# Modulation weights stored by tiles, one block's products moved ahead of the last of them, and a last down projection that alternates its two experts

## The chip, the cores and the metric

The kernel runs on one core of a Trainium2 chip. The metric is the device time of one execution in microseconds (us). The median of three runs before the change is 1856.98 us (1856.57 to 1857.13).

## What is computed

Two layers over 512 latent tokens and 256 context tokens of width 1024, all in float32:

```
for l in range(2):
    mod = silu(c) @ w_ada[l] + b_ada[l]          # 1024 x 6144: shift, scale, gate, twice; the same for c_ctx
    xn  = rms(x) * g1 * (1 + scale1) + shift1
    u   = xn @ w_in[l]                           # q, k, v, gates | conv a, g | fourier
    x   = x + gate1 * (mixers(u) @ w_out[l])     # mLSTM, Conformer convolution, Fourier mixing
    xn2 = rms(x) * g2 * (1 + scale2) + shift2
    # 16 experts, each takes its 64 latent (32 context) tokens of highest affinity
    x   = x + gate2 * sum_e P_e (silu(xs @ Wg[e]) * (xs @ Wu[e])) @ Wd[e] * affinity
return rms(x) * g_final
```

The context rows run through layer 0 in full; layer 1 needs only their keys, values and gates.

## The kernel before

Feature blocks of 128 stand on the partitions, tokens on the free axis. SBUF is one large tile `A` that the kernel divides by hand, with `RA`, `RB` and six `WP` tiles beside it; `PS` is PSUM, eight banks. PE's order is that of the code, written out by hand. The instructions of the other engines are set in order by a scheduler, and each engine runs its own in order. SP issues nearly all weight loads; GpSimd's queue (POOL) issues the modulation weights except the first 16 tiles, the fetches of scan tables (`scr`) and the indirect gathers and scatters.

**Modulation weights.** `w_ada` is 2 x 1024 x 6144. A tile is 128 rows of it by four pieces of 256 columns (512 KB), and in the array as it is given each row of a tile lies in four runs of 1 KB. There are 96 tiles: 16 in `ada_first` (SP, line 309), 32 in `ada0` and 48 in `ada1` (POOL, line 282, in `ada_round`). Four products of 32 columns each (`cs`, lines 284 and 311) take a tile, one for each column group of the array.

**The start.** `ada_first` makes shift and scale for layer 0 in two halves. The first half gives feature blocks 0, 1, 4, 5; the second gives 2, 3, 6, 7. `KORD` sets the blocks' order to match, and `normed` makes each block's two-part normalized input on ACT and DVE (lines 505 to 510). Two columns of `w_in` are multiplied block by block as they come (`steps`, line 490, 12 products a block). Seven of the eight tiles of the second half stand ahead of the first block (`ADP`); `ADF` says after which block the eighth, with the rows and the selection behind it (lines 316 to 325), stands.

**The middle of layer 0.** Around 330 us the output projection begins. SP has by then queued the zeroing of the two accumulators (`accl`, `accc`) and, in memory that this zeroing reads from, the router's weights (`w_router`, line 1104). DVE scales these (line 1108) ahead of its first residual update (line 1177), which frees PE's banks. POOL loads tiles of `w_ada` for layer 1 in the same stretch.

**The experts of layer 1.** Pairs of experts; each of gate, up and down of a pair takes eight 1 MB tiles. 16 buffers hold them, and SP loads a tile when its buffer is free. In `wide` (line 1433) the two experts' products alternate, expert 0 in columns 0 to 63 of the array and expert 1 in 64 to 127. The last pair's down projection is `down_last`: four quarters (`qd`) of 256 output features. In each quarter the products stand in runs of four of one expert (line 1693), with a scatter (`pop(scat)`: two products of line 1498 and DVE's update, line 1499) behind a run. After a quarter ACT and DVE take its half bank out as a high and a low part (lines 1699 and 1700), and two more scatters are queued; `last_sum` adds the squares (line 1675) whose sums (`rows`, line 1683) give the final norm (line 356 on).

A float32 product is two records in the profile, so 16 products of a quarter are 32 records.

Of the kernel before, what the change touches and what calls it, by code (L numbers as in the profile page):

```python
# [15 lines left out]
KB = 8  # L16
# [29 lines left out]
LEARLY = 6  # L46
ADP, ADF = 7, (2, 0, 0, 0)
CR0, CR1 = 0.75, 1.1
# [107 lines left out]
def build(nc, tc, xT, ctxT, params, w_ada, w_gates, w_in, w_out, w_router, w_e_gate, w_e_up, w_e_down,  # L156
# [3 lines left out]
    pe, act, dve, pool, sp = nc.tensor, nc.scalar, nc.vector, nc.gpsimd, nc.sync  # L160


    def body(A, RB, PS, scr, xrow, acc):
# [112 lines left out]
        def ada_round(l, r, ring, bank, eng, firsts=(), some=1):  # L276
            ps = B(bank)
            src = w_ada[l].rearrange("(k p) (r g h c) -> r h k p g c", p=128, r=3, g=4, h=2)
            for hf in range(2):
                for k in range(KB):  # L280
                    w = V(ring.next(), 4, 256)
# [19 lines left out]
        def ada_first(ring, bank, bank2, eng, splits):  # L301

            ps = B(bank)
            src = w_ada[0].rearrange("(k p) (r g h c) -> r h k p g c", p=128, r=3, g=4, h=2)[0]
            p2 = B(bank2)[:, 0:32].rearrange("p (b v g) -> p b v g", b=4, v=2)
# [91 lines left out]
        for l in range(2):  # L397
# [734 lines left out]
            wq = [(w, 2 * q + e, i) for w, q in order for i in range(4) for e in range(2)]  # L1132
            wtiles, wtaken = [], [0]

            def load_experts(firsts=(), most=1000):
                while len(wtiles) < min(wtaken[0] + len(wreg), len(wq), most):
                    w, e, i = wq[len(wtiles)]
                    if last and w is w_e_down and e >= E - 2:
                        t = V(wreg[len(wtiles) % len(wreg)], KB, 256)
                        src = w[l, e, i].rearrange("p (k c) -> p k c", k=KB)  # L1140

                        for k0, k1 in ((0, KB),) if i < 3 else ((0, 4), (4, KB)):
                            sp.dma_start(t[:, k0:k1], src[:, k0:k1])
                    else:
                        t = V(wreg[len(wtiles) % len(wreg)], 2, D)
                        r = sp.dma_start(t, w[l, e, i].rearrange("p (a f) -> p a f", a=2))
                        after(r, firsts)
                    wtiles.append(t)
# [91 lines left out]
            p = B(3)  # L1240
# [216 lines left out]
            def pop(lst, n=1):  # L1457
                for _ in range(min(n, len(lst))):
                    lst.pop(0)()
# [202 lines left out]
            def down_last(p):  # L1662
# [23 lines left out]
                for qd in range(4):  # L1686
                    w = wtiles[wtaken[0]:wtaken[0] + 2]
                    wtaken[0] += 2
                    b = B(o + qd // 2)[:, qd % 2 * 256:qd % 2 * 256 + 256]
                    for k0 in (0, 4):  # L1690
                        for e in range(2):
                            for k in range(k0, k0 + 4):
                                pe.matmul(b[64 * e:64 * e + 64], hT[:, k, 64 * e:64 * e + 64], w[e][:, k],  # L1693
                                          start=k == 0, stop=k == KB - 1, tile_position=(0, 64 * e))
                            pop(scat)
                    pop(scat, 99)
                    c0 = qd * 256
                    h, lo = (YS[:, j, c0:c0 + 256] for j in range(2))
                    act.activation(h, b, AF.Copy, scale=GP[:, 0, p:p + 1])
                    dve.scalar_tensor_tensor(lo, b, GP[:, 0, p:p + 1], h.bitcast(F32), op0=OP.mult, op1=OP.subtract)  # L1700
                    if qd == 2:
                        rows(range(4))
                    scat.extend(last_sum(db) for db in (2 * qd, 2 * qd + 1))
                rows((4, 5))
# [58 lines left out]
def layout(inputs):  # L1763
# [30 lines left out]
    a["params"] = par  # L1794
    a["w_ada"] = f("w_ada")
    a["w_gates"] = wg.reshape(2, 128, KB * 32)
# [48 lines left out]
```

## Time and profile before

| | |
|---|---|
| median of 3 runs | 1856.98 us |
| the profiled execution's own time | 1857.74 us |
| its span (first to last instruction) | 1856.0 us |
| PE busy | 1744.3 us, 94% |
| DVE busy | 627.9 us, 34% |
| ACT busy | 448.5 us, 24% |
| POOL busy | 166.0 us, 9% |
| moved by DMA | 529.59 MB, mean 285 GB/s |

The busy shares are means over stages with different limits, so the stages are read one by one: what PE waits for at the start, around 360 us and at the end, and when the DMA engines have no room left.

### The profile page before, as it was taken

What the parts mean: (1) busy time and instruction counts of PE and PEld (TensorE: products, weight loads), DVE (VectorE), ACT (ScalarE), POOL (GpSimd) and SP (SyncE); (2) the same over time, 40 slices, a digit from 0 to 9 for tenths busy, and PEclk for the clock granted to TensorE, in tenths of its full rate; (3) what the DMA queues carried; (4) which work ended last, traced back from release to release, by engine and by line L of the source; (5) the groups of instructions that cost most, each with busy time, mean ns of one, the idle gap of its engine ahead of it and who ended that gap; (6) DMA issues with size and microseconds to landing.
All of it is one profiled execution on the core that took longest, in us unless ns stands there. A gap on an engine that the chain in (4) does not pass through costs nothing.

```text
span 1856.0 us, 27692 instructions
## 1 busy us (share of the span) xinstructions
PE 1744.3 (94%) x11728; PEld 947.8 (51%) x11728; DVE 627.9 (34%) x1384; ACT 448.5 (24%) x862; POOL 166.0 (9%) x193
## 2 busy tenths in 40 slices
PE   7899999899899999999999989889989999999997
PEld 3678887676333333333233468777644444334433
DVE  4624897323201001001014567956230221121213
ACT  5423354313201101101000553346221001110001
POOL 1122120321101101101100001110000000000000
PEclk8999999899899999999999999999989999999998
DMA  9365344855899999999995112233659999999992
GB/s 346 115 208 193 106 133 137 314 188 209 350 419 402 411 412 403 399 421 391 393 393 217 35 54 79 76 108 129 250 240 421 420 420 421 420 421 420 421 420 99
DMA packets 100668, 529.59 MB, mean 285 GB/s; under 512 B 10176, under 2 KB 21440, under 8 KB 51648
## 3 DMA queue, kind: packets, MB, share of 16 engines
q1 hardware_dynamic: 81920, 459.66, 61.8%
q0 software_dynamic: 18624, 68.17, 11.7%
q8 instruction: 92, 1.51, 0.3%
q14 instruction: 32, 0.26, 0.0%
HBM read 513.10 MB, written 14.68 MB: 284 GB/s over the span
## 4 chain that ended last, share of the span: by engine, by line
PE 70%; DMA 10%; DVE 9%; issue 5%; ACT 2%; SPq 2%; POOL 1%; another core or an unknown queue 0%; DVEq 0%; POOLq 0%; ACTq 0%
PE PS L1433 29%; PE PS L490 16%; PE PS L1443 8%; PE PS L1379 3%; DVE A L1015 2%; PE PS L1498 2%; PE PS L284 1%; PE PS L1693 1%; SPq L309 1%; DMA accc<-A 1%; DMA WP<-w_e_up 1%; DMA A<-w_e_up 1%; DMA A<-w_e_down 1%; DMA A<-w_e_gate 1%; DMA WP<-w_e_gate 1%
## 5 line engine op out<-in xcount | busy, mean ns | idle before, releaser
L490 PE MATMUL PS<-RA,RB 128*128 128x512 f32 (+1 forms) x2352 | 516.4, 367 | 23.6 <-ACT A L973 8.0
L1433 PE MATMUL PS<-A 128*32 128x512 f32 (+1 forms) x2256 | 428.1, 594 | 2.7 <-DMA A<-w_e_up 2.2
L490 PEld LDWEIGHTS PS<-RA,RB 128*128 128x128 f32 x2352 | 379.3, 194 | 99.3 <-issue 20.6
L1433 PE MATMUL PS<-WP,A 128*32 128x512 f32 (+1 forms) x2160 | 373.9, 597 | 0.7 <-DMA WP<-w_e_up 0.7
L1433 PEld LDWEIGHTS PS<-A 128*32 128x32 f32 (+1 forms) x2256 | 128.0, 121 | 224.9 <-issue 213.7
L1433 PEld LDWEIGHTS PS<-WP,A 128*32 128x32 f32 (+1 forms) x2160 | 107.0, 117 | 192.7 <-issue 187.6
L1443 PE MATMUL PS<-WP,A 128*32 128x512 f32 x816 | 112.5, 595 | 0.0
L1015 DVE SCALAR_TENSOR_TENSOR A<-A 128x783 f32<-128x783 f32 (+1 forms) x120 | 107.4, 921 | 0.1
L1499 DVE SCALAR_TENSOR_TENSOR A<-PS,A 128x512 f32<-128x512 f32 x80 | 57.5, 748 | 130.5 <-PE PS L1498 130.5
L1387 ACT ACTIVATE A<-PS,A 128x128 f32<-128x128 f32 x80 | 36.4, 457 | 262.0 <-DVE A L1389 260.8
L1486 ACT ACTIVATE A<-PS 128x512 f32<-128x512 f32 x40 | 23.8, 597 | 306.2 <-PE PS L1485 306.0
L1389 DVE TENSOR_SCALAR A<-PS,A 128x128 f32<-128x128 f32 x80 | 32.6, 409 | 185.8 <-PE PS L1382 93.4
L1443 PE MATMUL PS<-A 128*32 128x512 f32 x656 | 95.3, 607 | 0.0
L422 ACT ACTIVATE RB<-A 128x1024 fp32r<-128x1024 f32 x60 | 63.2, 1057 | 128.4 <-PE PS L490 83.1
L1532 DVE TENSOR_SCALAR A<-PS,A 128x512 f32<-128x512 f32 x6 | 4.5, 750 | 245.6 <-PE PS L1433 245.6
L282 POOL DMA_DIRECT2D A<-w_ada x80 | 60.1, 754 | 211.2 <-PE PS L284 134.2
L1506 DVE SCALAR_TENSOR_TENSOR RB<-PS,A,RB 128x512 fp32r<-128x512 f32 x18 | 13.5, 750 | 163.7 <-ACT RB L1505 162.8
L1379 PE MATMUL PS<-A 128*128 128x128 f32 x512 | 64.0, 285 | 5.0 <-DVE A L1499 4.5
L425 DVE TENSOR_TENSOR RB<-A,RB 128x1024 fp32r<-128x1024 f32 x50 | 60.8, 1221 | 21.0 <-ACT RB L422 20.6
L1379 PEld LDWEIGHTS PS<-A 128*128 128x128 f32 x512 | 61.0, 199 | 12.9 <-DVE A L1499 9.8
L1443 PEld LDWEIGHTS PS<-WP,A 128*32 128x32 f32 x816 | 26.8, 109 | 50.8 <-issue 50.8
L1498 PE MATMUL PS<-RB 128*128 128x512 f32 x160 | 51.7, 431 | 1.0 <-DVE A L1499 0.4
(334 smaller groups left out, 1583.8 us busy)
## 6 DMA issues: line engine op xcount, KB each, us to landing
A<-w_e_gate SPq DMA_DIRECT2D x75, 1024.0 KB, 14.3
A<-w_e_up SPq DMA_DIRECT2D x66, 1024.0 KB, 13.0
WP<-w_e_down SPq DMA_DIRECT2D x63, 1024.0 KB, 14.3
A<-w_e_down SPq DMA_DIRECT2D x63, 1024.0 KB, 16.0
WP<-w_e_up SPq DMA_DIRECT2D x62, 1024.0 KB, 13.0
WP<-w_e_gate SPq DMA_DIRECT2D x53, 1024.0 KB, 14.9
A<-w_ada POOLq DMA_DIRECT2D x80, 512.0 KB, 5.5
A<-w_in SPq DMA_DIRECT2D x44, 512.0 KB, 3.7
```

The costliest lines, as they stand in the source:

```text
L282: after(eng.dma_start(w, src[r, hf, k]), firsts if hf == 0 and k < len(ring.regs) else ())
L422: whi.append(act.activation(h, raw[i], AF.Copy))
L425: wlo.append(eng.tensor_tensor(lo, raw[i], h.bitcast(F32), OP.subtract))
L490: pe.matmul(banks[s][:, :LEN[s]], w[:, k], xin[:, j, k, OFF[s]:OFF[s] + LEN[s]], start=k == k0 and i == 0, stop=k == k1 and i == 2)
L1015: dve.scalar_tensor_tensor(o, i, wcol, o, op0=OP.mult, op1=OP.add)
L1379: pe.matmul(b[:, j], XT[2 + c][:, db * 128:db * 128 + 128], onehots[i][:, c], start=c == 0, stop=c == 3)
L1387: act.activation(dst[:, db], b[:, j], AF.Identity, bias=sh_, scale=sc_)
L1389: dve.tensor_scalar(dst[:, db], b[:, j], sc_, sh_, op0=OP.mult, op1=OP.add)
L1433: pe.matmul(B(o + hf)[c:c + wd, :], lhs(k, e)[:, c % 64:c % 64 + wd], w[e][:, a, hf * 512:hf * 512 + 512], start=k == 0, stop=k == KB - 1, ...
L1443: pe.matmul(B(o + 2)[32 * g:32 * g + 32, :], lhsc(k, e), w[e][:, a, hf * 512:hf * 512 + 512], start=k == 0, stop=k == KB - 1, tile_positio ...
L1498: pe.matmul(b, YS[:, j, db * 128:db * 128 + 128], PM if pm is None else pm, start=j == 0, stop=j == 1)
L1499: dve.scalar_tensor_tensor(X[LAT][:, db], b, MOD[l][:, LAT, 40 + db:41 + db], X[LAT][:, db], op0=OP.mult, op1=OP.add)
```

## The change

`w_ada` is laid out on the host so that a tile is contiguous: 128 rows of 4 KB. Its loads name the same tiles, buffers and queues. At the start the eighth tile of the second half, and what hangs on it, stands after the second feature block's products and not after the first's. In `down_last` the two experts alternate product by product; the scatters stand behind the quarter's evacuation (in the first quarter, where the ones left from the pair before are taken, ahead of it); `rows(range(4))` stands after the fourth quarter's products; and the last quarter's weights are loaded as first halves of both experts, then second halves.

```diff
-ADP, ADF = 7, (2, 0, 0, 0)
+ADP, ADF = 7, (0, 2, 0, 0)
...
         def ada_round(l, r, ring, bank, eng, firsts=(), some=1):
             ps = B(bank)
-            src = w_ada[l].rearrange("(k p) (r g h c) -> r h k p g c", p=128, r=3, g=4, h=2)
+            src = w_ada[l].rearrange("r h k p (g c) -> r h k p g c", g=4)
...
         def ada_first(ring, bank, bank2, eng, splits):
-            src = w_ada[0].rearrange("(k p) (r g h c) -> r h k p g c", p=128, r=3, g=4, h=2)[0]
+            src = w_ada[0, 0].rearrange("h k p (g c) -> h k p g c", g=4)
...
-                        for k0, k1 in ((0, KB),) if i < 3 else ((0, 4), (4, KB)):
-                            sp.dma_start(t[:, k0:k1], src[:, k0:k1])
+                        halves.append((t, src))
+                        if i < 3:
+                            sp.dma_start(*halves.pop())
+                        elif len(halves) == 2:
+                            for k0 in (0, 4):
+                                for t_, s_ in halves:
+                                    sp.dma_start(t_[:, k0:k0 + 4], s_[:, k0:k0 + 4])
...
-                    for k0 in (0, 4):
+                    for k in range(KB):
                         for e in range(2):
-                            for k in range(k0, k0 + 4):
-                                pe.matmul(b[64 * e:64 * e + 64], hT[:, k, 64 * e:64 * e + 64], w[e][:, k],
-                                          start=k == 0, stop=k == KB - 1, tile_position=(0, 64 * e))
-                            pop(scat)
-                    pop(scat, 99)
+                            pe.matmul(b[64 * e:64 * e + 64], hT[:, k, 64 * e:64 * e + 64], w[e][:, k],
+                                      start=k == 0, stop=k == KB - 1, tile_position=(0, 64 * e))
                     c0 = qd * 256
                     h, lo = (YS[:, j, c0:c0 + 256] for j in range(2))
+                    if qd == 0:
+                        pop(scat, 99)
                     act.activation(h, b, AF.Copy, scale=GP[:, 0, p:p + 1])
                     dve.scalar_tensor_tensor(lo, b, GP[:, 0, p:p + 1], h.bitcast(F32), op0=OP.mult, op1=OP.subtract)
-                    if qd == 2:
+                    if qd == 3:
                         rows(range(4))
+                    pop(scat, 99)
                     scat.extend(last_sum(db) for db in (2 * qd, 2 * qd + 1))
...
-    a["w_ada"] = f("w_ada")
+    a["w_ada"] = np.ascontiguousarray(f("w_ada").reshape(2, KB, 128, 3, 4, 2, 256).transpose(0, 3, 5, 1, 2, 4, 6)).reshape(2, 3, 2, KB, 128, 1024)
```

PE's rows in the second quarter of `down_last`, before (L1693 are the quarter's products, `WP1` and `WP2` the weights of expert 0 and expert 1, L1498 a scatter):

```order
L1693 MATMUL PS_70<-WP1_8538,A_63 64x256 x4
L1498 MATMUL PS_70<-RB_64 128x512 x2
L1693 MATMUL PS_70<-WP2_8539,A_63 64x256 x4
L1498 MATMUL PS_70<-RB_64 128x512 x2
L1693 MATMUL PS_70<-WP1_8538,A_63 64x256 x4
L1693 MATMUL PS_70<-WP2_8539,A_63 64x256 x4
```

The same quarter now (the products are L1699, a scatter is L1504; the pair of rows repeats eight times), from the scatters behind the first quarter to the start of the third:

```order
L1504 MATMUL PS_70<-RB_64 128x512 x4
L1699 MATMUL PS_70<-WP1_8538,A_63 64x256
L1699 MATMUL PS_70<-WP2_8539,A_63 64x256
...
L1504 MATMUL PS_70<-RB_64 128x512 x4
L1699 MATMUL PS_70<-WP3_8540,A_63 64x256
L1699 MATMUL PS_70<-WP4_8541,A_63 64x256
```

Runs of four became an alternation, and both scatters of a quarter stand together behind it.

DVE's rows from the up projection of the last pair to the final norm, before (L1700 is the low part of a quarter, L1499 the update behind a scatter):

```order
L1477 TENSOR_TENSOR A<-PS,A 128x512 x2
L1499 SCALAR_TENSOR_TENSOR A<-PS,A 128x512 x4
L1700 SCALAR_TENSOR_TENSOR RB<-PS,A,RB 128x256
L1499 SCALAR_TENSOR_TENSOR A<-PS,A 128x512 x2
L1700 SCALAR_TENSOR_TENSOR RB<-PS,A,RB 128x256
...
L1499 SCALAR_TENSOR_TENSOR A<-PS,A 128x512 x2
L370 RECIPROCAL A<-A 128x4
```

And now (L1707 and L1505 are the same two):

```order
L1483 TENSOR_TENSOR A<-PS,A 128x512 x2
L1505 SCALAR_TENSOR_TENSOR A<-PS,A 128x512 x4
L1707 SCALAR_TENSOR_TENSOR RB<-PS,A,RB 128x256
L1505 SCALAR_TENSOR_TENSOR A<-PS,A 128x512
L1707 SCALAR_TENSOR_TENSOR RB<-PS,A,RB 128x256
L1505 SCALAR_TENSOR_TENSOR A<-PS,A 128x512 x2
L1707 SCALAR_TENSOR_TENSOR RB<-PS,A,RB 128x256
L1505 SCALAR_TENSOR_TENSOR A<-PS,A 128x512
L1707 SCALAR_TENSOR_TENSOR RB<-PS,A,RB 128x256
L1505 SCALAR_TENSOR_TENSOR A<-PS,A 128x512 x4
L370 RECIPROCAL A<-A 128x4
```

Four updates, not two, now stand behind the last low part, and the third low part stands behind the first update of its own quarter's scatters.

PE's rows at the start, before, between the first block's products and the second's (L490 are the blocks' products, L311 the eighth tile's, L319 the selection):

```order
L490 MATMUL PS<-RA,RB 128x256
L490 MATMUL PS<-RA,RB 128x512
L311 MATMUL PS<-A 32x256 [waits DMAHW7_49]
L311 MATMUL PS<-A 32x256 x3
L319 MATMUL PS<-A 128x8 [waits Activation_49]
L319 MATMUL PS<-A 128x8
```

The same rows now stand behind the second block's 12 products, whose first rows follow on the first block's:

```order
L490 MATMUL PS<-RA,RB 128x256 [waits Activation_49]
L490 MATMUL PS<-RA,RB 128x512
L490 MATMUL PS<-RA,RB 128x256 [waits DVE_49]
...
L311 MATMUL PS<-A 32x256 [waits DMAHW7_49]
L311 MATMUL PS<-A 32x256 x3
L319 MATMUL PS<-A 128x8 [waits Activation_49]
```

12 products that wait for ACT and DVE alone moved ahead of the wait for the eighth tile.

## Rows read from the trace of the kernel before

**Rows 1.** Page, part 2: GB/s in 40 equal slices of the span.

```profile
GB/s 346 115 208 193 106 133 137 314 188 209 350 419 402 411 412 403 399 421 391 393 393 217 35 54 79 76 108 129 250 240 421 420 420 421 420 421 420 421 420 99
```

**Rows 2.** Chain that ended last: start us, us, what.

```profile
350.88 7.25 DMA A<-w_router
...
1476.58 20.75 PE PS L1433 x96
...
1767.65 19.85 DMA A<-w_e_up
```

**Rows 3.** Timeline of PE at the start: start us, us, engine, instructions, [idle before <-releaser].

```profile
37.99 2.03 PE L490 MATMUL PS<-RA,RB 128*128 128x256 f32 x10 [0.16 <-DVE RA L510]
41.19 0.64 PE L311 MATMUL PS<-A 128*32 128x256 f32 x8 [1.17 <-DMA A<-w_ada]
...
42.80 8.72 PE L490 MATMUL PS<-RA,RB 128*128 128x256 f32 x48
```

**Rows 4.** Timeline of DVE at the start.

```profile
36.33 1.94 DVE L510 TENSOR_TENSOR RA<-A,RA 128x512 fp32r<-128x512 f32 x4
...
45.71 0.92 DVE L510 TENSOR_TENSOR RA<-A,RA 128x256 fp32r<-128x256 f32 x2 [0.20 <-ACT A L507]
```

**Rows 5.** Timeline around 360 us.

```profile
358.22 0.76 DVE L1108 TENSOR_TENSOR A<-A 128x256 f32<-128x256 f32 x2 [17.59 <-DMA A<-w_router]
...
360.09 2.93 PE L490 MATMUL PS<-RA,RB 128*128 128x256 f32 x9 [4.39 <-DVE A L1177]
```

**Rows 6.** POOL's DMA queue, 320 to 365, 360 to 440, 446 to 481: packets, MB, share.

```profile
q0 software_dynamic: 2016, 7.34, 44.2%
...
q0 software_dynamic: 3400, 12.34, 47.1%
...
q0 software_dynamic: 718, 2.62, 22.9%
```

**Rows 7.** Timeline of the last down projection, all engines.

```profile
1804.02 1.94 PE L1693 MATMUL PS<-A 128*64 128x256 f32 x8
1805.89 0.73 PE L1498 MATMUL PS<-RB 128*128 128x512 f32 x2
1806.73 0.75 DVE L1499 SCALAR_TENSOR_TENSOR A<-PS,A 128x512 f32<-128x512 f32 x1 [3.50 <-PE PS L1498]
...
1810.22 0.38 PE L1693 MATMUL PS<-A 128*64 128x256 f32 x1
1810.28 0.38 PE L1693 MATMUL PS<-WP,A 128*64 128x256 f32 x1
1810.44 0.38 PE L1693 MATMUL PS<-A 128*64 128x256 f32 x1
...
1812.05 0.47 ACT L1699 ACTIVATE RB<-PS,A 128x256 fp32r<-128x256 f32 x1 [7.42 <-PE PS L1693]
1812.56 0.48 DVE L1700 SCALAR_TENSOR_TENSOR RB<-PS,A,RB 128x256 fp32r<-128x256 f32 x1 [2.54 <-ACT RB L1699]
1813.10 1.49 PEld L1693 LDWEIGHTS PS<-WP,A 128*64 128x64 f32 x8 [1.60 <-DVE RB L1700]
...
1839.47 1.29 ACT L1675 ACTIVATE A<-A 128x512 f32<-128x512 f32 x2 [2.01 <-DVE A L1499]
...
1841.90 0.60 ACT L356 ACTIVATE A<-PS 128x512 f32<-128x512 f32 x1 [1.14 <-PE PS L1683]
```

**Rows 8.** SP's issues of the last weights, and the halves' size and median landing time.

```profile
1799.94 4.03 SPq L1143 DMA_DIRECT2D A<-w_e_down  x2
...
A<-w_e_down SPq DMA_DIRECT2D x2, 512.0 KB, 15.0
```

**Rows 9.** Stretches at the end: us, PE, PEld, DVE, ACT, POOL, granted clock, DMA, GB/s.

```profile
1840.00:1845.00 5.00, 2.76 (x12) 1.24 (x12) 1.00 (x6) 1.59 (x4) 0.00 (x0) 0.95 0.00 0
1845.00:1850.00 5.00, 2.04 (x2) 0.50 (x2) 2.77 (x6) 0.00 (x0) 0.00 (x0) 0.50 0.19 70
```

**Rows 10.** Line 1693 alone: ns min/median/max of one, first and last start.

```profile
L1693 PEld LDWEIGHTS PS<-WP,A x96: 132/137/137, 1806.6 to 1835.4; 128*64 128x64 f32 x96
```

More of the change, by code (lines that the diff above doesn't have):

```diff
@@ L1132, in body @@
             wq = [(w, 2 * q + e, i) for w, q in order for i in range(4) for e in range(2)]
-            wtiles, wtaken = [], [0]
+            wtiles, wtaken, halves = [], [0], []
             def load_experts(firsts=(), most=1000):
```

## The prediction

> **What bounds the kernel now.** I read the GB/s row first. From slice 31 to 39 it stands at 420: the experts of layer 1 are fed as fast as the DMA engines go [rows 1]. The chain of waits says who loses time there: through the experts it runs on PE at first, and later on transfers, one of 19.85 us per eight tiles [rows 2]. SP starts a load when a buffer is free and PE frees buffers, so this whole stretch starts where PE's earlier work ends: a microsecond saved before it is a microsecond saved at the end, as long as it is on PE's path. So three places are read apart: the start, the stretch around 360 us, and the last down projection, where the transfers run out and PE, ACT and DVE set the end alone.
>
> **The start.** PE finishes the first block's products at 37.99 + 2.03 = 40.02 and then idles until 41.19, 1.17 us of it for a tile of `w_ada`; from 41.19 to 42.80 the eighth tile, its copy by ACT and its selection take 1.61 us; then products run dense, 48 in 8.72, 2.18 a block [rows 3]. The second block's input is ready at 36.33 + 1.94 = 38.27 [rows 4], so its products can run from 40.02 to 42.2 and cover the wait for the tile (41.15) whole. The 1.61 us stay bare behind them, 42.2 to 43.8. The third block then starts at 43.8 and not at 42.80 + 2.18 = 44.98: 1.17 us saved. What hides the edit is thin: the fifth block's input, ready at 45.71 + 0.92 = 46.6 [rows 4], comes 1.0 later (47.6), and PE wants it at 43.8 + 2 x 2.18 = 48.2, 0.6 us of cover. If tiles of 4 KB rows land sooner, the wait is gone anyway; the two edits do not add up. Bounds: nothing (if the cover fails by 1.2) to 1.2. I take 1.17.
>
> **The modulation weights.** Bytes, queues and buffers stay, only the runs in DRAM grow. Off PE's path this costs and gives nothing: POOL's loads elsewhere are early. On the path it has one place. PE stands 4.39 us until 360.09 behind DVE, which stands behind the router's weights [rows 5]; these took 7.25 us to land for 128 KB [rows 2], as POOL's queue took 44.2% of the DMA engines' time from 320 to 365, 19.9 us, for 7.34 MB, nearly all `w_ada` [rows 6]. A cheaper `w_ada` lets the zeroing and the router's weights land sooner. No row shows `w_ada` in 4 KB rows. From below: POOL's gathers of 4 KB rows cost 22.9% of 35 us x 16 / 718 = 0.179 us a packet, `w_ada` now 47.1% of 80 us x 16 / 3400 = 0.177, both of some 3.6 KB [rows 6]: nothing gained. From above: at 420 GB/s [rows 1] the 7.34 MB take 17.5 us, 2.4 less; and if the chain were quite free, the whole 4.39. A loss I exclude: no transfer grows. The gathers are the nearest row, but they go from row to row at random places, so I take a little more than their nothing: 0.8.
>
> The Trainium skill (DMA: Bandwidth & Descriptors, Specifications) gives 512 B as the smallest transfer that reaches line rate. By that, runs of 1 KB are already there and this term would be 0. The row of the gathers agrees, as far as it goes.
>
> **The last down projection.** Count from the first product, 1804.02. Now four products of one expert take 1805.89 - 1804.02 = 1.87 us [rows 7]. Where a run of one expert meets the next, the two interleave: records of the two buffers start at 1810.22, 1810.28, 1810.44, so a pair of records takes 0.215 us where one expert alone takes 0.23 a record [rows 7]. Line 1433, which alternates throughout, holds that rate: 96 records of 512 columns in 20.75 us, 0.216 each, twice what one column group could do [rows 2]. So a quarter of 32 records takes 16 x 0.215 = 3.44; I take 3.5, against 4 x 1.87 = 7.5.
>
> Then the hand-overs. A scatter takes 0.73 us (two in a row 1.2, as the second starts under the first); its update starts 0.84 after it and takes 0.75; ACT starts 0.1 behind a quarter, DVE 0.51 later, and PE goes on in the same bank 0.54 after that (1812.05, 1812.56, 1813.10) [rows 7]. With DVE's new order:
> - Quarter 0: 0 to 3.5; two old scatters to 4.7; their updates 4.34 to 5.85; low part at 5.87; PE waits for it (same bank) until 6.41.
> - Quarter 1: to 9.91, scatters to 11.1. Quarter 2 has another bank and starts at once: to 14.6, scatters to 15.8, first update 15.44 to 16.19, low part 16.21, PE at 16.75.
> - Quarter 3: to 20.25; four row sums to 21.15; scatters to 22.35; updates to 23.5; squares (1.29 for two [rows 7]) to 24.2. Here the new order costs: the next row sums stand ahead of the last scatters in PE's queue, so scatter 6 starts at 25.1; updates to 27.45, last square 28.15, and the norm 1.14 later (1839.47 + 1.29 = 1840.76 to 1841.90 now [rows 7]): 29.3.
>
> Now the norm starts at 1841.90 - 1804.02 = 37.88. The tail gains 8.6.
>
> Do weights arrive in time? The last half is issued at 1803.6 and lands 15.0 later, at 1818.6, or 14.6 in this count [rows 8]; quarter 3 wants it at 16.75 or later. At 2.5 us per MB before it (420 GB/s), quarter 2's last tile is there at 9.6 for 11.1, quarter 1's at 4.6 for 6.4. Covers of 1.5 us and more; a later tile would cost what it is late beyond that. The order of the halves hides under this and is worth nothing. The tail's bounds: 7.1, if PE's granted clock falls to 1.2 GHz about 3 us earlier than now (it stands at 0.95 and then 0.50 at the end [rows 9]) and the last scatters and sums double; 9.2, if the row sums cost less than 0.9.
>
> **Sum.** 1.17 + 0.8 + 8.6 = 10.6. The profiled execution took 1857.74: 1847.2. It lies 0.76 above the median of the runs, 1856.98, so the forecast for the median is 1846.4.
>
> **Rivals.**
> 1. *The layout gives nothing.* The gathers' price speaks for it. Only the 0.8 is lost: 1847.2.
> 2. *PE's wait at 360 goes whole.* DVE waited 17.59 us for that transfer [rows 5], in a stretch where the queue is full; against it, `w_ada`'s share would have to shrink by a fifth. 4.4 for 0.8: 1842.8.
> 3. *Weight loads bind the alternation.* A product's load of 64 columns takes 0.135 us [rows 10], and 32 of them 4.3 us, more than 3.44. If loads did not overlap across the column groups, each quarter would cost 0.9 more, 3.5 in all: 1849.9. Against it, in the interleaved records two loads pass in 0.215 [rows 7]. The Trainium skill (TensorE: Matmul & The Clock Gate, Part 3, Measured speedup) has three column tiles at 2.38 and not 3 times. At that efficiency an estimate for a quarter is 3.44 / 0.79 = 4.35, and the time about the same; line 1433 here shows none of that loss.
> 4. *The alternation does not overlap at 256 columns, and switching groups costs as a run does now.* Place: the four quarters. Price: 7.5 for 3.5 each, 16 us, so that the tail loses 7.3: 1862.3. It decides from a quarter of 3.5 + 10.6 / 4 = 6.15 us on. The three interleaved records speak against it; for it only that no full quarter of this form has been seen.
> 5. *The change misses its mark*: the rows of the new order show that it is made, so this is left to rivals 1 and 4.
>
> **How the numbers follow.** Forecast 0.60, rivals 1 to 4: 0.15, 0.08, 0.10, 0.05; 0.02 for mixtures that end near no change. The likeliest gives 1846.4, with its own bounds 1844 to 1849.3 (tail 7.1 to 9.2, start 0 to 1.2, middle 0.3 to 2.4). The range takes in rivals 1 to 3: 1842.0 to 1850.5. It leaves out rival 4 and the mixtures. What a measurement can tell from no change is about 0.2%, 3.7 us. All cases but the last two are faster by more: 0.92 after a little for what I have not seen, 0.03 the same, 0.05 slower.
>
> **What would show it.** PE's timeline at the start: no wait for `w_ada` behind the first block, 12 more products there, the second row sums for the gates 1.2 earlier (if the wait stands, the start was wrong). The wait behind the router's weights: 3 to 4.4 us if rival 1 or the forecast is right, gone by rival 2. In the last down projection: 32 records in 3.4 to 3.6 us; PE idle some 1.7 us ahead of the second quarter and 1 us ahead of the fourth, both for DVE's low part; the norm some 29 us behind the first product; no wait for `w_e_down`. A quarter of 4.3 is rival 3, of 7 rival 4. The prediction is wrong most likely in the tail, if a wait for the last weights takes the place of PE's work, or at 360 us, where one transfer's landing decides.

## The result, and the profile after

The changed kernel takes 1848.18 us (median of five executions, 1842.92 to 1849.08), the kernel before 1857.13 beside it (five, 1856.57 to 1861.64): ratio over all executions 0.993, 95% interval 0.9903 to 0.9958 (the two medians alone give 0.9952). It is faster; the forecast was 1846.4, a ratio of 0.9943 to the 1856.98 shown then. The profiled execution takes 1848.78 with a span of 1847.0, 9.0 less than before.

Where these 9.0 us stand is read from stations that both traces have:

| station | before | after | after minus before |
|---|---|---|---|
| second row sums for the gates (L516) | 59.44 | 60.34 | +0.90 |
| PE behind the wait at 360 (L490) | 360.09 | 361.79 | +1.70 |
| an up projection of layer 1 (L1433, now L1439) | 1476.58 | 1476.80 | +0.22 |
| first product of the last down projection (L1693, now L1699) | 1804.02 | 1804.17 | +0.15 |
| final norm (L356) | 1841.90 | 1833.23 | -8.67 |
| end of the span | 1856.0 | 1847.0 | -9.0 |

So between these two executions all of it comes from the tail, and what lies ahead of it gives nothing. The chain of waits of the kernel after (start us, us, what) has the same links as in [rows 2]:

```profile
353.80 6.03 DMA A<-w_router
...
1476.80 20.75 PE PS L1439 x96
...
1767.78 19.86 DMA A<-w_e_up
```

The transfers of layer 1 are as full as in [rows 1], 420 in slices 31 to 39 (page, part 2):

```profile
GB/s 347 112 209 191 106 123 155 301 203 177 341 420 402 410 413 403 404 418 401 391 406 259 35 39 93 62 108 113 239 222 422 420 421 420 420 420 421 420 421 179
```

**The last down projection.** Timeline of the kernel after; L1699 are the products, L1504 scatters, L1505 their updates, L1706 and L1707 the high and low parts, L1689 row sums:

```profile
1804.44 0.38 PE L1699 MATMUL PS<-A 128*64 128x256 f32 x1
1804.44 0.38 PE L1699 MATMUL PS<-WP,A 128*64 128x256 f32 x1
1804.65 0.38 PE L1699 MATMUL PS<-A 128*64 128x256 f32 x1
1804.66 0.38 PE L1699 MATMUL PS<-WP,A 128*64 128x256 f32 x1
...
1807.78 1.20 PE L1504 MATMUL PS<-RB 128*128 128x512 f32 x4
1808.62 1.41 DVE L1505 SCALAR_TENSOR_TENSOR A<-PS,A 128x512 f32<-128x512 f32 x2 [5.23 <-PE PS L1504]
1810.47 3.67 PE L1699 MATMUL PS<-WP,A 128*64 128x256 f32 x32 [1.50 <-DVE RB L1707]
...
1815.20 3.67 PE L1699 MATMUL PS<-WP,A 128*64 128x256 f32 x32
...
1820.77 0.43 PE L1699 MATMUL PS<-WP,A 128*64 128x256 f32 x1 [0.77 <-DVE RB L1707]
...
1833.23 0.60 ACT L356 ACTIVATE A<-PS 128x512 f32<-128x512 f32 x1 [1.14 <-PE PS L1689]
```

Records of the two experts start in pairs 0.215 apart, and the 32 of a quarter take 3.67. Counted from 1804.17, PE goes on at 6.30 behind DVE's low part, at 11.03 without a wait, and at 16.60 behind DVE again; the norm stands at 29.06, where [rows 7] had 37.88. No row here waits for a transfer: SP's last issue of a half is at 1802.61 (1803.6 before, [rows 8]).

```profile
1802.61 0.33 SPq L1149 DMA_DIRECT2D A<-w_e_down  x1
```

**The start.** PE's timeline after, against [rows 3]:

```profile
32.63 0.64 PE L311 MATMUL PS<-A 128*32 128x256 f32 x8 [0.55 <-DMA A<-w_ada]
34.98 1.08 PE L311 MATMUL PS<-A 128*32 128x256 f32 x8 [1.71 <-DMA A<-w_ada]
37.49 1.08 PE L311 MATMUL PS<-A 128*32 128x256 f32 x8 [1.43 <-DMA A<-w_ada]
38.50 5.79 PE L490 MATMUL PS<-RA,RB 128*128 128x256 f32 x24
44.22 0.64 PE L311 MATMUL PS<-A 128*32 128x256 f32 x8
...
60.34 1.50 PE L516 MATMUL PS<-A 128*32 128x256 f32 x16
```

The eighth tile, at 44.22, is waited for no longer: that is the edit. But PE now waits 3.7 us for three tiles ahead of it, and the first 24 products behind them take 5.79, begun at a lower granted clock (0.50 from 35 to 40 us). These waits were not in the forecast.

**Around 360 us.** Timeline, then POOL's queue from 320 to 365 (packets, MB, share), against [rows 5, 6]:

```profile
359.92 0.76 DVE L1108 TENSOR_TENSOR A<-A 128x256 f32<-128x256 f32 x2 [16.61 <-DMA A<-w_router]
...
361.79 2.93 PE L490 MATMUL PS<-RA,RB 128*128 128x256 f32 x9 [5.59 <-DVE A L1183]
```

```profile
q0 software_dynamic: 2016, 7.34, 40.3%
```

The same 7.34 MB take 40.3% where they took 44.2%, and the router's weights land in 6.03 and not 7.25; but PE's wait is longer, 5.59 for 4.39: the zeroing ahead of these weights was issued at 331.72, 2.7 later than before (329.04), PE's own work only some 0.5 later.

### The profile page after: what moved, and what is told of

It reads as the page before. It is cut to its first block, busy times and chain, and to the rows that moved or that the text cites. A ratio compares the mean times of both kernels' runs of the same rounds, so it can differ in the third digit from the quotient of the medians.

```text
span 1847.0 us, 27691 instructions
## 1 busy us (share of the span) xinstructions
PE 1729.1 (94%) x11728; PEld 939.8 (51%) x11728; DVE 626.9 (34%) x1384; ACT 448.3 (24%) x862; POOL 147.8 (8%) x193
## 4 chain that ended last, share of the span: by engine, by line
PE 70%; DMA 11%; DVE 9%; issue 6%; ACT 2%; POOL 1%; another core or an unknown queue 0%; SPq 0%; DVEq 0%; POOLq 0%; ACTq 0%
PE PS L1439 29%; PE PS L490 16%; PE PS L1449 9%; PE PS L1385 3%; DVE A L1015 2%; PE PS L1504 2%; PE PS L284 1%; DMA A<-w_ada 1%; DMA accc<-A 1%; DMA A<-w_e_gate 1%; DMA A<-w_e_up 1%; DMA WP<-w_e_gate 1%; DMA A<-w_e_down 1%; DMA WP<-w_e_up 1%; DMA WP<-w_e_down 1%
## 5 line engine op out<-in xcount | busy, mean ns | idle before, releaser
L490 PE MATMUL PS<-RA,RB 128*128 128x512 f32 (+1 forms) x2352 | 516.9, 367 | 26.0 <-ACT A L973 7.7
L490 PEld LDWEIGHTS PS<-RA,RB 128*128 128x128 f32 x2352 | 379.7, 194 | 101.9 <-issue 20.0
L1439 PE MATMUL PS<-A 128*32 128x512 f32 (+1 forms) x2256 | 427.7, 594 | 2.7 <-DMA A<-w_e_up 2.2
L1439 PE MATMUL PS<-WP,A 128*32 128x512 f32 (+1 forms) x2160 | 372.6, 595 | 0.6 <-DMA WP<-w_e_up 0.6
L1439 PEld LDWEIGHTS PS<-A 128*32 128x32 f32 (+1 forms) x2256 | 127.8, 121 | 225.0 <-issue 214.5
L1439 PEld LDWEIGHTS PS<-WP,A 128*32 128x32 f32 (+1 forms) x2160 | 106.7, 117 | 191.5 <-issue 186.7
L1505 DVE SCALAR_TENSOR_TENSOR A<-PS,A 128x512 f32<-128x512 f32 x80 | 57.3, 747 | 128.9 <-PE PS L1504 128.9
L282 POOL DMA_DIRECT2D A<-w_ada x80 | 42.4, 533 | 221.2 <-PE PS L284 140.6
L1504 PE MATMUL PS<-RB 128*128 128x512 f32 x160 | 50.6, 428 | 1.0 <-DVE A L1505 0.4
```

The costliest lines, as they stand in the source:

```text
L282: after(eng.dma_start(w, src[r, hf, k]), firsts if hf == 0 and k < len(ring.regs) else ())
L490: pe.matmul(banks[s][:, :LEN[s]], w[:, k], xin[:, j, k, OFF[s]:OFF[s] + LEN[s]], start=k == k0 and i == 0, stop=k == k1 and i == 2)
L1439: pe.matmul(B(o + hf)[c:c + wd, :], lhs(k, e)[:, c % 64:c % 64 + wd], w[e][:, a, hf * 512:hf * 512 + 512], start=k == 0, stop=k == KB - 1, ...
L1504: pe.matmul(b, YS[:, j, db * 128:db * 128 + 128], PM if pm is None else pm, start=j == 0, stop=j == 1)
L1505: dve.scalar_tensor_tensor(X[LAT][:, db], b, MOD[l][:, LAT, 40 + db:41 + db], X[LAT][:, db], op0=OP.mult, op1=OP.add)
```

## The experiments

Executions differed more in these groups than in the first one (the kernel before: 1847.88 to 1864.67), so a ratio is to be read with its interval. Positions are those of the one profiled execution of each kernel: the start of the second row sums for the gates (59.44 before), and the norm counted from the first product of the last down projection (37.88 before).

| run | executions | median | before beside it | ratio (95%) | row sums at | norm |
|---|---|---|---|---|---|---|
| tail | 10 | 1846.85 | 1854.72 | 0.9959 (0.9942 to 0.9977) | 65.86 | 29.06 |
| layout | 12 | 1851.68 | 1854.72 | 0.9974 (0.9961 to 0.9988) | 58.56 | 37.87 |
| order | 12 | 1855.22 | 1854.72 | 1.0002 (0.9985 to 1.0019) | 58.29 | 37.87 |
| head | 12 | 1849.62 | 1854.72 | 0.997 (0.9955 to 0.9984) | 57.92 | 37.88 |
| after2 | 6 | 1842.63 | 1856.44 | 0.9935 (0.9913 to 0.9956) | 56.77 | 29.05 |
| hold | 6 | 1840.66 | 1856.44 | 0.9921 (0.9896 to 0.9945) | 56.90 | 29.05 |
| holdt | 6 | 1840.35 | 1856.44 | 0.9922 (0.9902 to 0.9941) | 58.30 | 29.04 |
| runs | 7 | 1846.68 | 1856.44 | 0.9953 (0.9931 to 0.9975) | 58.18 | 33.13 |
| holdb | 12 | 1850.34 | 1855.85 | 0.9971 (0.9959 to 0.9984) | 57.66 | 37.88 |
| hold_mid | 4 | 1836.13 | 1855.85 | 0.9893 (0.9877 to 0.991) | 56.08 | 26.97 |
| hold_end | 5 | 1840.77 | 1855.85 | 0.9922 (0.9908 to 0.9937) | 56.30 | 25.36 |
| old_mid | 4 | 1840.22 | 1856.8 | 0.9913 (0.9893 to 0.9934) | 57.66 | 26.98 |

### Each part alone

**tail**: the edits of `load_experts` and `down_last` alone.

```diff
-                    for k0 in (0, 4):
+                    for k in range(KB):
                         for e in range(2):
...
+                    pop(scat, 99)
                     scat.extend(last_sum(db) for db in (2 * qd, 2 * qd + 1))
```

> The kernel before with the new last down projection alone (alternation, moved scatters and row sums, order of the last halves). Theory A (the whole gain is the tail; the start and the middle gave nothing that reaches the end): the norm 29.1 us behind the first product of the last down projection, against 37.9 before, and a time 8.8 us below the kernel before, ratio 0.9953, so the same as the changed kernel's profiled execution. Theory B (the parts add as predicted, and the profiled execution of the changed kernel lost 2 us of it by chance): 8.6 below, and the changed kernel's median 2 us better than this one.

The norm is at 29.06, and the ratio is worth 7.6 us of 1854.72 (4.3 to 10.8): the tail's 8.8 lies in it. It does not tell whether the rest gives 0 or 2.

**layout**: the three lines of `w_ada` alone.

```diff
-            src = w_ada[l].rearrange("(k p) (r g h c) -> r h k p g c", p=128, r=3, g=4, h=2)
+            src = w_ada[l].rearrange("r h k p (g c) -> r h k p g c", g=4)
```

> The kernel before with the modulation weights laid out by tiles alone. Theory A: in the first 45 us the transfers run at 415 to 420 GB/s instead of 381 to 402, the first half of ada_first's products ends about 3.5 us earlier, but GpSimd's queue then starts its four tiles earlier too and the second half's tiles come no earlier: the second row sums for the gates stand at 59.4 us plus or minus 1 (before 59.4), the time is that of before within 1 us. Theory B: the start gains 1.2 us (no wait for the eighth tile) and the middle 0.8: 2 us below the kernel before, second row sums at 58.2.

A falls here: the time is 4.8 us lower (2.2 to 7.2), more than B's 2 too. Its one profile shows 0.9 of it at the row sums.

**order**: `ADF` alone.

```diff
-ADP, ADF = 7, (2, 0, 0, 0)
+ADP, ADF = 7, (0, 2, 0, 0)
```

> The kernel before with the eighth tile behind the second block alone, the weights in the old layout. Transfers at the start are as before, so both theories want the second row sums for the gates 1.2 us earlier, at 58.3 us. Theory A: most of that is swallowed before the last stage (a stretch at the lower clock level between 95 and 100 us that ends at the same time, waits on transfers at 235 and 310 us): 0 to 0.6 us below the kernel before. Theory B: 1.2 us below.

The row sums are 1.15 earlier, as both theories wanted; the time is that of before, within 0.2%, which does not tell the theories' 0 to 0.6 and 1.2 us apart.

**head**: layout and order, without the tail.

> The kernel before with layout and order, the last down projection as before. Theory A: the start is that of the changed kernel, second row sums at 60.3 us, PE waiting 3 to 4 us for tiles of the second half between 31 and 38 us; first product of the last down projection at 1804 us as before, time that of before within 1 us. Theory B: the row sums at 58.2 us, first product of the last down projection 2 us earlier, time 2 us below the kernel before.

Row sums 1.5 earlier, time 5.6 us lower (3.0 to 8.3): theory A took the 60.34 and the 1804 of one execution for the kernel's. Tail and head together make 13.2, and the changed kernel again (below) 12.1. Within their intervals the parts add; it is the size of the layout's part that I had wrong, and the profiles had to say why one execution can lose what others gain.

### What varies at the start

The profiled executions at hand differ there. The two that show it best both have the old layout. Timeline of PE, then of POOL, of the kernel with the new tail alone:

```profile
25.96 2.57 PE L311 MATMUL PS<-A 128*32 128x256 f32 x32
...
32.59 0.64 PE L311 MATMUL PS<-A 128*32 128x256 f32 x8 [0.70 <-DMA A<-w_ada]
37.12 1.08 PE L311 MATMUL PS<-A 128*32 128x256 f32 x8 [3.89 <-DMA A<-w_ada]
41.08 1.08 PE L311 MATMUL PS<-A 128*32 128x256 f32 x8 [2.88 <-DMA A<-w_ada]
...
65.86 1.50 PE L516 MATMUL PS<-A 128*32 128x256 f32 x16
...
28.41 1.69 POOL L282 DMA_DIRECT2D A<-w_ada  x2 [26.38 <-PE PS L311]
```

And of the kernel with the new order alone:

```profile
29.45 3.29 PE L311 MATMUL PS<-A 128*32 128x256 f32 x32
...
33.82 3.37 PE L311 MATMUL PS<-A 128*32 128x256 f32 x56
...
32.53 1.68 POOL L282 DMA_DIRECT2D A<-w_ada  x2 [30.51 <-DMA A<-w_ada]
```

In the first, the first half's last products start at 25.96, buffers come free, and GpSimd issues its first tiles of `w_ada` at 28.41, while SP's second half is still on its way. Tiles that came 1.34 us apart (31.25 and 32.59) then come 4.5 and 4.0 apart. In the second, the same products start at 29.45, GpSimd issues at 32.53, and PE waits for no tile. What parts the two is the granted clock (stretches of the first, then of the second; columns as in [rows 9]):

```profile
15.00:20.00 5.00, 2.39 (x21) 1.22 (x22) 1.11 (x5) 2.14 (x3) 0.00 (x0) 1.00 1.09 385
20.00:25.00 5.00, 3.36 (x38) 2.01 (x29) 3.40 (x14) 0.53 (x2) 0.00 (x0) 0.89 1.07 404
...
35.00:40.00 5.00, 1.08 (x8) 0.20 (x8) 4.13 (x9) 4.09 (x8) 0.13 (x1) 0.50 1.04 360
```

```profile
15.00:20.00 5.00, 2.39 (x13) 1.20 (x8) 0.65 (x3) 2.14 (x3) 0.00 (x0) 0.86 1.09 386
20.00:25.00 5.00, 5.00 (x39) 2.42 (x38) 2.74 (x8) 0.00 (x0) 0.00 (x0) 0.50 1.07 403
```

PE was busy 2.39 of 5 us from 15 to 20 in both; in one its clock stayed at 2.4 GHz to 20 us, in the other it fell to 1.2 GHz, where it stayed from 20 to 25. The faster PE finishes its work sooner, so GpSimd's tiles collide with the second half, and the row sums stand 7.6 us later (65.86 for 58.29, 1.15 of which is the order). The profile of the changed kernel is of the first course, that of the kernel before of the second. The two are the ends of a range: over all fourteen profiles, the first half's last products start between 25.69 and 29.45. Among the eight without the hold (below), PE then waits 6.8 us for two tiles where they start at 25.96 (old layout), 3.7 for three at 25.69, 1.55 at 26.74, 1.23 at 27.80 (new layout), and at most 0.2 from 29.16 on (the eighth tile left aside).

How much of a collision reaches the end, no profile tells. The kernel with the new tail alone has the kernel before's code up to the last down projection. Chain of waits (start us, us, what), before and then there:

```profile
435.64 4.37 PE PS L490 x24
...
1014.67 4.43 PE PS L1621 x40
```

```profile
441.73 4.37 PE PS L490 x24
...
1014.30 4.43 PE PS L1627 x40
...
1472.99 20.75 PE PS L1439 x96
```

It is 6.1 us later at 441.73, but 0.4 earlier at 1014.30 and 3.6 earlier at 1472.99 (1476.58 in [rows 2]), and this execution, 1845.29, is shorter than its kernel's median, 1846.85. From DVE's row that stood at 460.06 before to that at 1035.21, a stretch without modulation weights that no edit touches, the profile before takes 575.15, this one 568.69, the other twelve 570.4 to 572.9. So single executions differ behind the start by several us, for reasons that stay open, and what the start is worth has to be read from the times of many.

**after2**: the changed kernel again.

> The changed kernel itself, beside the others of this call. Theory A (the start takes one of two courses: where TensorE keeps its higher clock between 15 and 25 us, the first half's products end 3.5 us earlier, GpSimd's four tiles start then and hold up the second half's tiles; where the clock falls there, they start behind them): a time of about 0.993 of the kernel before; the second row sums for the gates either near 57.9 us (clock low at 20 to 30 us) or near 60.3 us (clock high at 15 to 25 us). Theory B (course and time of the start are a matter of the layout alone): near 57.9 in any case.

0.9935, as A expected, and 56.77 at the row sums: a course between the two, with GpSimd's first issue at 30.21 and one wait of 1.23 us. That fits neither A's two positions nor B's claim that the layout alone sets the course.

**hold**: GpSimd's first four tiles wait for SP's last tile of the second half. **holdb** is the same edit in the kernel before, **holdt** in the kernel with the new tail alone.

```diff
-                    eng.dma_start(w, src[hf, k])
+                    adal[:] = [eng.dma_start(w, src[hf, k])]
...
-                            yield from ada_round(0, r, Ring(areg), 5, pool, wloads[1:2] if r == 1 else (), some=ADS[0])
+                            yield from ada_round(0, r, Ring(areg), 5, pool, wloads[1:2] + adal if r == 1 else (), some=ADS[0])
```

> The changed kernel, and GpSimd's first four tiles of modulation weights wait until SP's last tile of the second half has landed. Theory A: no wait of PE for tiles of the second half in either course, second row sums for the gates at 57.9 us or earlier, GpSimd's tiles landed by 45 us and not wanted before 64 us; 1 to 3 us below the changed kernel and with less spread between executions. Theory B: GpSimd's four tiles are not what delays the second half; waits of PE for them of 3 to 4 us remain where the clock stays high, and the time is that of the changed kernel within 1 us.

0.9921 for 0.9935: some 2 us less, which six executions cannot tell from nothing. The spread that A wanted smaller is not: 1835.29 to 1845.06, for 1838.82 to 1845.29 without the hold. PE's timeline has no wait for a tile, GpSimd issues at 36.49, and the row sums stand at 56.90.

> The kernel before with the new last down projection, and GpSimd's first four tiles held in the same way: modulation weights in the old layout and the old order. Theory A: the layout's gain over the kernel before (4.8 us by the run with the layout alone) came mostly from the course in which GpSimd's tiles collide with the second half's; with them held, this kernel is 2 to 5 us below the one with the new last down projection alone, and no more than 1 to 2 us above the held kernel in the new layout. Theory B: the layout gains its 3 to 5 us elsewhere; this kernel stays that much above the held kernel in the new layout.

0.9922 against 0.9959 without the hold, 6.9 us, more than A's 2 to 5 (the two stood in different groups, each beside the kernel before), and no more than the held kernel in the new layout (0.9921). A's direction holds; by this pair, layout and order are worth nothing in time once the tiles are held.

> The kernel before, with nothing changed but that GpSimd's first four tiles of modulation weights wait for SP's last tile of the second half. Theory A (the median of the kernel before holds executions in which those four tiles collide with the second half's, and the layout's gain of 4.8 us was mostly the mending of that): 3 to 5 us below the kernel before, second row sums for the gates at 59.5 us or earlier. Theory B (the layout gains elsewhere, in transfers): within 1 us of the kernel before.

5.4 us below the kernel before (3.0 to 7.6), by an edit that moves no byte and no product, only the issue of four tiles. The time is A's. That it comes from executions with a collision is argued, not shown: the one profile of the kernel before has none, and it is not known how many of its executions do. PE's timeline, and POOL's issue:

```profile
27.03 3.62 PE L313 MATMUL PS<-A 128*32 128x256 f32 x32
...
33.83 0.64 PE L313 MATMUL PS<-A 128*32 128x256 f32 x8 [0.20 <-DMA A<-w_ada]
35.17 0.64 PE L313 MATMUL PS<-A 128*32 128x256 f32 x8 [0.70 <-DMA A<-w_ada]
36.54 0.64 PE L313 MATMUL PS<-A 128*32 128x256 f32 x8 [0.73 <-DMA A<-w_ada]
...
57.66 1.50 PE L518 MATMUL PS<-A 128*32 128x256 f32 x16
...
38.17 3.18 POOL L282 DMA_DIRECT2D A<-w_ada  x4 [3.36 <-DMA A<-w_ada]
```

An early first half (27.03) is now followed by tiles 1.35 apart, and the row sums come 8.2 earlier than in the colliding execution, 1.8 earlier than in the other course. In all six profiles with the hold they stand between 56.08 and 58.30; in the eight without it between 56.77 and 65.86.

### What the alternation is worth

**runs**: the changed kernel with runs of four of one expert again.

```diff
-                    for k in range(KB):
+                    for k0 in (0, 4):
                         for e in range(2):
+                            for k in range(k0, k0 + 4):
```

> The changed kernel, with the products of each quarter of the last down projection in runs of four of one expert again; scatters, row sums and the halves of the weights stay where the change put them. Theory A (the alternation is what makes a quarter 3.6 us and not 7.5): the norm 29.1 + 4 x 3.9 = 44.7 us behind the first product, later than the 37.9 of the kernel before, and 15.6 us above the changed kernel. Theory B (the moved scatters and row sums carry a good part of the tail's gain): the norm at 34 us or less.

Theory A is off by far, and B holds: the norm is at 33.13. Timeline of PE:

```profile
1809.53 4.70 PE L1700 MATMUL PS<-WP,A 128*64 128x256 f32 x32 [1.49 <-DVE RB L1708]
1814.16 1.20 PE L1504 MATMUL PS<-RB 128*128 128x512 f32 x4
1815.29 4.70 PE L1700 MATMUL PS<-WP,A 128*64 128x256 f32 x32
```

Four runs of 1.87 each would be 7.5, but they take 4.70: where runs of the two experts meet, 0.93 us of one goes under the other, three times a quarter. Before, scatters stood on two of these three seams. So with the scatters out of the quarters the alternation gives 4.07 (33.13 - 29.06, four times the 1.03 between 4.70 and 3.67), and the scatters and row sums, moved first, give 4.75 (37.88 - 33.13). In the other order the shares are different, as the next run shows.

**hold_mid**: the held kernel, the two scatters behind the fourth pair of products.

```diff
                             pe.matmul(b[64 * e:64 * e + 64], hT[:, k, 64 * e:64 * e + 64], w[e][:, k],
                                       start=k == 0, stop=k == KB - 1, tile_position=(0, 64 * e))
+                        if k == 3:
+                            pop(scat, 2)
+                    pop(scat, 99)
...
-                    if qd == 3:
+                    if qd == 2:
                         rows(range(4))
-                    pop(scat, 99)
```

> The held kernel in the new layout, with the last down projection's products alternating as in the change, but the scatters in the middle of a quarter (behind the fourth pair of products) and the row sums where the kernel before had them. Theory A (a scatter costs its own 0.6 us wherever it stands, and what the kernel before lost was the overlap of one expert's run with the next, which the scatters between the runs cut): a quarter with two scatters in it takes 3.7 + 1.2 + 0.2 = 5.1 us, PE waits only 1.1 us ahead of the second and fourth quarters, and the norm comes 27.5 to 28.5 us behind the first product, a little earlier than the changed kernel's 29.1. Theory B (a scatter inside a quarter costs the alternation far more than its own time, because PE drains around it): a quarter of 6 us or more, the norm at 31 us or later.

A quarter takes 4.95 with its scatters, as A wanted, and the norm is at 26.97, half a us better than A's range. This is the fastest of all: 0.9893, faster than the changed kernel's 0.9935 (0.9913 to 0.9956); against the held kernel, from which it differs by these places alone, the intervals overlap (0.9921, 0.9896 to 0.9945). PE's timeline, third quarter:

```profile
1806.84 1.40 PE L1506 MATMUL PS<-RB 128*128 128x512 f32 x4
1808.17 1.95 PE L1701 MATMUL PS<-WP,A 128*64 128x256 f32 x16
```

Half a quarter takes 1.95 and two scatters their 1.20 to 1.40: a scatter in the midst of an alternation costs its own time only. So the alternation, with the scatters still inside the quarters and the row sums where they were, brings the norm from 37.88 to 26.97, 10.9 us, and moving scatters and row sums out as the change did costs 2.1 of that (29.05). The two edits take away the same loss, the missing overlap of the runs; neither has a share of its own.

**hold_end**: the held kernel, old scatters ahead of the first quarter, last scatters ahead of the last row sums.

```diff
+                    if qd == 0:
+                        pop(scat, 99)
                     for k in range(KB):
...
-                    if qd == 0:
-                        pop(scat, 99)
                     act.activation(h, b, AF.Copy, scale=GP[:, 0, p:p + 1])
...
-                rows((4, 5))
                 pop(scat, 99)
-                rows((6, 7))
+                rows((4, 5, 6, 7))
```

> The held kernel in the new layout, with two places of the new last down projection put right where my forecast saw a cost: the two scatters left from the pair before stand ahead of the first quarter and not behind it, and the last two scatters stand ahead of the last four row sums. Theory A: PE waits 1.1 us for the first quarter's evacuation instead of 2.7 us with the scatters, and the end no longer has two rounds of scatter, squares and row sums in a row; the norm 26 us behind the first product, 3 us earlier than in the changed kernel, and the time 3 us below the held kernel. Theory B: the scatters in front delay the first product by as much as they free behind it, and DVE's updates are the bound at the end: the norm no earlier against the end of the up projection than now, time as the held kernel.

The norm is at 25.36, but the first product comes 1.3 later behind the scatters, so against the end of the up projection 2.4 are gained (29.54 from DVE's last row of it, for 31.92). Of that, the time shows nothing, as B wanted (0.9922 for the held kernel's 0.9921). The span goes on 14.07 behind the norm and not 13.11, but that need not be the edit: among the other profiles, too, some go on 13.1 (layout) and some 14.07 (the kernel before) with the same code there. The rest I cannot find in executions that differ by 5.

### Is the layout worth anything once nothing collides?

**old_mid**: hold_mid with `w_ada` in the old layout.

```diff
-            src = w_ada[0, 0].rearrange("h k p (g c) -> h k p g c", g=4)
+            src = w_ada[0].rearrange("(k p) (r g h c) -> r h k p g c", p=128, r=3, g=4, h=2)[0]
```

> The held kernel with the scatters in the middle of the quarters, and with it the new order at the start, but the modulation weights in the old layout. Theory A (the layout is worth something only where GpSimd's four tiles collide with the second half's; elsewhere it gains 0.6 us around 360 us and loses 1.5 us between 225 and 255 us, where the fetch of a scan table lands later): the stretch from the scan table's selection to the residual update that followed at 255.34 in the kernel before takes 30.6 to 31.0 us as in every profile with the old layout, and the time is that of the same kernel in the new layout, 1836.1, within 2 us. Theory B (the layout is worth 2 us or more by itself): 1838 us or later against a kernel before of 1856.

The stretch takes 30.64, as A wanted, but the median is B's. By ratios the layout is worth 3.7 us, with intervals that overlap; the profiles show where 1.6 of it is. PE's timeline in old_mid, then in hold_mid:

```profile
35.35 0.64 PE L313 MATMUL PS<-A 128*32 128x256 f32 x8 [0.72 <-DMA A<-w_ada]
36.72 0.64 PE L313 MATMUL PS<-A 128*32 128x256 f32 x8 [0.73 <-DMA A<-w_ada]
```

```profile
33.78 0.64 PE L313 MATMUL PS<-A 128*32 128x256 f32 x8 [0.59 <-DMA A<-w_ada]
35.00 0.64 PE L313 MATMUL PS<-A 128*32 128x256 f32 x8 [0.59 <-DMA A<-w_ada]
```

PE waits for each of these tiles in both; they come 1.37 apart in runs of 1 KB, 1.22 in rows of 4 KB, and the row sums stand at 57.66 and 56.08. So A is wrong in its "only where they collide" at the row sums. What that is worth in time stays between nothing (hold against holdt) and these 3.7.

## Why the prediction was right, and where not

**The tail** was right in its steps, and it is the greater part of the gain. Forecast and measured, from the first product: PE behind the first wait 6.41 and 6.30, third quarter 11.1 and 11.03, fourth 16.75 and 16.60, norm 29.3 and 29.06; a quarter 3.5 and 3.67; gain 8.6 and 8.8. What I said of its cause was half of it: I priced a quarter of runs at 4 x 1.87 = 7.5 and so ascribed all to the alternation. The 7.5 supposes runs that never overlap; where no scatter stands between them they do, and a quarter takes 4.70. The alternation is worth 10.9 with the scatters left inside the quarters, 4.07 with them moved out.

**The rivals.** Rival 3 (weight loads bind) is out: a pair of records passes in 0.215. The efficiency that the Trainium skill (TensorE: Matmul & The Clock Gate, Part 3, Measured speedup) gives for three column tiles, 2.38 for 3, does not show with two tiles of 64 columns here: one expert alone takes 0.23 a record [rows 7], the two together 0.215 a pair. Rival 4 is out, as a quarter takes 3.67; its price of 16 rests on the same 7.5, and undoing the alternation costs 4.07. Rival 2 did not come: PE waits 5.59 at 360. Rival 1 named the layout as worthless; by the time of the layout alone (4.8 us, 2.2 to 7.2) it is not, but what shows of it lies at the start, where neither the rival nor the forecast looked.

**The start** is the step that failed, in the sentences "If tiles of 4 KB rows land sooner, the wait is gone anyway; the two edits do not add up" and "Bounds: nothing to 1.2". The order's own term was right: 1.15 by the order alone, 1.17 forecast. What I left out is that the layout touches this stretch, too, and that the stretch depends on when GpSimd's first four tiles start. I read one profile, of the course without a collision, and took its waits for the kernel's. Where they collide, the new layout ends 4.4 us sooner than the old (65.86 - 60.34, less 1.15 for the order); where PE keeps its clock and they don't, 1.6; where the clock falls, 0.1 to 0.4 (58.29 in the old, 58.18 and 57.92 in the new). The time says 4.8 for the layout. Holding the four tiles takes 5.4 out of the kernel before. How often executions collide, which would tie these numbers to the medians, is not shown, and neither is that they reach the end: in the one profile with the long collision they don't. So the prediction's "a microsecond saved before it is a microsecond saved at the end" is not shown for the start, and the 4.8 and the 5.4 have a cause that is argued.

**The middle** came near the forecast where I looked and went wrong where I didn't. From DVE's row that stood at 339.41 before to that at 389.60, six profiles in the old layout take 50.12 on the mean and eight in the new 49.54, 0.6 less for 0.8 forecast; but the eight lie between 47.67 and 52.51, so this is not told from nothing. And between two rows of DVE that stood at 224.71 and 255.34 before, the new layout takes 32.24 on the mean (30.86 to 33.35), the old 30.70 (30.63 to 30.96): 1.5 lost. PE's rows behind the scan table there, before and in the changed kernel's second profile:

```profile
236.18 1.67 PE L490 MATMUL PS<-RA,RB 128*128 128x256 f32 x9 [0.47 <-ACT A L1038]
```

```profile
235.17 1.20 PE L490 MATMUL PS<-RA,RB 128*128 128x256 f32 x7 [2.30 <-ACT A L1038]
```

The fetch of the table lands 7.8 us after its issue before, 10.0 there. "Off PE's path this costs and gives nothing" did not hold: no tile of `w_ada` is on its way then, and what makes the fetch slower is open.

**The total.** The tail gives 8.8 in all five profiles that have it as changed (norm at 29.04 to 29.06). What is left for the head is 0.2 by the medians of the first group (8.95) and 5.0 by those of the second (13.8), 3 to 4 by the two ratios (0.993 and 0.9935, 13.0 and 12.1 us). The forecast's 10.6 was 8.6 and 2.0: the tail right, the head's sum near the middle of these, but made of terms of which the start's was too small by the time of the layout, and the middle's, by the two stretches read, had the wrong sign. That the head's sum came out near is luck. One bound was added up wrong: 7.1 + 0 + 0.3 leave 1849.6, not 1849.3; the range does not hang on it.

## What to carry to other kernels

Where transfers of two queues meet, ask what releases the second one: an engine that gets faster upstream can release it into the first one's way, and an edge that holds it back may be worth as much as faster transfers (5.4 us here for four tiles, 4.8 for the layout). One profile is one course: where a granted clock stands at a half for some slices, look at what would move if it did not, and do not take a difference of two single traces for that of two kernels. And before a sequence is reordered, measure it without what stands between its parts: two edits can take away the same loss, and the one made first seems to be worth most of it (10.9 or 4.75 of a gain of 8.8 here).

## What the runs showed of the hardware that was not expected

- Runs in DRAM far above 512 B are not equal: a 512 KB tile in runs of 1 KB came every 1.37 us (524288 B in it are 383 GB/s), in rows of 4 KB every 1.22 us (430 GB/s), on the same queue; the stretches from 15 to 35 us show 380 to 404 GB/s in the kernel with the new tail alone and 416 to 419 in the changed one. The tile became contiguous in the same step, so run length and distance of the rows changed together and no run parts them. The Trainium skill (DMA: Bandwidth & Descriptors, Specifications) has line rate from 512 B on; the trace differs by a tenth, and the trace decides.
- Runs of products on two column groups overlap where they meet, 0.93 us of 1.87, without any interleaving in the code (four runs in 4.70 us); with a scatter's two full-width products between them, as in the kernel before, they don't.
- Issuing tiles of 4 KB rows takes less of POOL's time: 1.05 us for two issues, where tiles in runs of 1 KB took 1.49 to 1.50.
